# A streaming encoder's MLP: loads at the change to the down product issued by need, and the next norm and the output rows placed inside the last down products' passes

## The chip, the cores and the metric

The kernel runs on one core of a Trainium2 chip. Its time is the device time of one execution in microseconds (us), taken as the median over several runs. Engines are named as the profile names them: PE is TensorE (PEld its weight loads), DVE is VectorE, ACT is ScalarE, POOL is GpSimd, SP is SyncE, whose queue issues nearly all DMA transfers. An instruction on an engine runs when those ahead of it on that engine have run, and when the work it waits for is done.

## The reference

One inference step of a two-layer streaming encoder on 1072 rows of 1024 features: 16 meta tokens, 32 sample rows and 1024 prompt rows. Layer 0 mixes with sliding-window attention beside gated linear attention, layer 1 with forgetting attention. Both layers end in the same MLP, which is what the change is about:

```python
def rmsnorm(x, g):
    xf = x.astype(jnp.float32)
    y = xf * lax.rsqrt(jnp.mean(xf * xf, axis=-1, keepdims=True) + EPS)
    return (y * g.astype(jnp.float32)).astype(x.dtype)

def mlp(h, w_up, w_down):          # w_up 1024 x 4096, w_down 4096 x 1024
    u = jax.nn.relu(h @ w_up)
    return (u * u) @ w_down
...
        xp = xp + mlp(rmsnorm(xp, norm_mlp[l]), w_up[l], w_down[l])
        xs = xs + mlp(rmsnorm(xs, norm_mlp[l]), w_up[l], w_down[l])
    y_prompt = xp[:, N_META:]
```

After layer 0 the rows go through the norm ahead of layer 1's projection; after layer 1 they are the outputs `y_sample` and `y_prompt`, in float32.

## The kernel before

**Layout.** `xT` holds all rows transposed: 128 partitions, 8 feature blocks, 1072 columns, one column for each row. The columns are worked on in four quarters (268 wide in layer 0; 264 in layer 1, which leaves out the meta tokens).

**Precision.** Each float32 product is made of three products of rounded parts: `hi_lo` casts an operand on ACT (line 64: the high part) and subtracts on DVE (line 66: the rest); `mm3` (lines 75 to 77) issues high·high, high·low and low·high. So every operand of TensorE costs one ACT cast and one DVE subtraction first.

**The MLP as seven products.** Each of the two matrix products is done as 2 x 2 blocks with seven block products (a Strassen form with sums S1 to S4 of weight blocks and T1 to T4 of activation blocks). The *up* product runs over 16 blocks of the hidden features; while it runs, `xT` is its scratch memory, so the residual has been spilled to `xsave` in DRAM, and its results go to `ud` in DRAM (the store of line 994). Its operands B11 and B21 lie in the pool `ho1`, the other five in `ho2`.

The *down* product (`down`, from line 1002) follows. For each of seven products n there are two column halves c, so 14 **passes**, written (n, c). A pass runs over 16 blocks kb of 128 hidden features, and for each over 4 output blocks ob with three matmuls: 192 matmuls, 128x268 in layer 0 and 128x264 in layer 1. Results gather in PSUM, in the tile called mu_y for c = 0 and bank for c = 1; at the end of a pass they are added into `xT` (line 1095). Products 0 to 3 give partial sums that go to several outputs; the lower feature half is complete after product 5 and the upper half in parts after products 4, 5 and 6.

**Operands of a pass.** A weight block is loaded as `md_raw` (256 KB, three buffers), combined with blocks that are kept in `md_k` (k1 = A11 and k2 = A21, 4 MB each), and split into `md_w`, one tile for each kb, for the next product while this product's second half runs. The activations come back from `ud` as `md_ur` (two kb at a time, called a group g here; three buffers) and are split into `md_u` (four buffers).

**Order.** TensorE's order inside the MLP is that of the code. Every other engine's order, SP's queue included, is set by a scheduler when the kernel is built.

**At the change to the down product** the code loads k1 (four loads of 1 MB), then for every kb the block A11 a second time as `md_raw` to make `md_w`, and during pass (0, 0) k2 and eight whole-width reloads `xT <- xsave`, two with each megabyte of k2.

**At the end.** In layer 0 the function `done` calls `norm` for quarters 0 and 1 after pass (5, 1), for quarter 2 after (6, 0) and for quarter 3 after (6, 1). `norm` squares the 8 feature blocks on ACT (line 129), adds them on DVE and POOL (line 131), takes the mean over features with one matmul against a constant matrix (line 138), and derives the factor from it; `scaled` then writes the split operand `h` of the projection. In layer 1 `store_rows` takes rows of `xT` through TensorE's transpose (line 1576), copies each half of the features out of PSUM, alternately with ACT (1578) and DVE (1580), and stores it (1581). This is done for the first 544 rows after pass (5, 1), and for 264 rows each after (6, 0) and (6, 1).

Of the kernel before, what the change touches and what calls it, by code (L numbers as in the profile page):

```python
# [8 lines left out]
F32 = mybir.dt.float32  # L9
# [9 lines left out]
P = 128  # L19
D = 1024  # L20
KB = 8
NMETA, NSAMP, NPROMPT = 16, 32, 1024
T = NMETA + NSAMP + NPROMPT
# [6 lines left out]
QMAX = 268  # L30
# [21 lines left out]
class Core:  # L52
# [64 lines left out]

    def squares(self, cols):
        nc, sb = self.nc, self.nm
        c0, c1 = cols  # L120
        w = c1 - c0
        x = self.xT[:, :, c0:c1]

        acc = [sb.tile([P, QMAX], F32, name=f"nm_acc{e}")[:, :w] for e in range(2)]
        for k in range(KB):
            e = k in (1, 3, 5)
            first = k < 2
            sq = acc[e] if first else sb.tile([P, QMAX], F32, name="nm_t", bufs=4)[:, :w]
            nc.scalar.activation(sq, x[:, k], AF.Square)
            if not first:  # L130
                (nc.gpsimd if e else nc.vector).tensor_tensor(acc[e], acc[e], sq, op=ALU.add)
        nc.vector.tensor_tensor(acc[0], acc[0], acc[1], op=ALU.add)
        return lambda: self.normed(w, acc[0])

    def normed(self, w, acc):
        nc, sb = self.nc, self.nm
        ps = self.bank()
        nc.tensor.matmul(ps[:, :w], self.mean, acc, start=True, stop=True)

        y, a = (sb.tile([P, QMAX], F32, name=f"nm_{x}")[:, :w] for x in "ya")  # L140
# [694 lines left out]
    def mlp_begin(self, l):  # L835
        self.l = l
        self.qs = QUARTERS[l]
        self.qw = self.qs[0][1] - self.qs[0][0]
        self.hw = 2 * self.qw
        self.ups = ExitStack()  # L840
        self.ho = {}
        self.operands("ho1", ("B11", "B21"))
        self.xsave = self.dram.tile([P, KB, T], F32, name=f"xsave{l}")

    def operands(self, name, which):
        pool = self.ups.enter_context(self.tc.tile_pool(name=name, bufs=1, side="right", reuse_waits="tile"))
        for x in which:
            self.ho[x] = pool.tile([P, 2, 4, self.hw], F32R, name=f"ho_{x}")
# [152 lines left out]

    def down(self, k1, k2, sb, ps, done):
        nc, i = self.nc, self.i
# [41 lines left out]
        def acts(n, c, g):  # L1045
# [22 lines left out]
        for n, c in passes:  # L1068
# [4 lines left out]
            for kb in range(NP):  # L1073
                if kb % 2 == 0:
                    ready(at)
                    u = us.pop(todo[at])
                    at += 1
                if n == 0 and c == 0 and kb % 4 == 0:
                    load(k2[:, kb:kb + 4], "A21", kb, 4)

                    o = kb // 4
                    for k in (2 * o, 2 * o + 1):
                        nc.sync.dma_start(self.xT[:, k, self.qs[0][0]:], self.xsave[:, k, self.qs[0][0]:])
                for ob in range(4):
# [13 lines left out]

    def mlp(self, after, done):

# [5 lines left out]
        with ExitStack() as st, tc.manual_schedule(engines={mybir.EngineType.PE}):  # L1106
            ps = st.enter_context(tc.tile_pool(name="mlp", bufs=4, space=PSUM, reuse_waits="tile"))
            self.nm = pool(st, "nml")
            self.operands("ho2", ("T4", "B22", "T3", "T2", "T1"))
            with tc.tile_pool(name="mu", bufs=1, reuse_waits="tile") as sb:  # L1110
# [8 lines left out]
            kp = pool(ks, "mk", "right")  # L1119
            k1, k2 = (kp.tile([P, self.NP, 512], F32, name=f"md_k{x}") for x in (1, 2))  # L1120
            sb = pool(st, "md")
            def end(n, c):
                if n == 5 and c == 1:
                    ks.close()
                    after()
                done(n, c)
            self.down(k1, k2, sb, ps, end)

# [439 lines left out]

    def store_rows(self, r0, m):
        nc, o = self.nc, self.o  # L1570
        dst = o["y_sample"][0] if r0 == 16 else o["y_prompt"][0, r0 - 48:r0 - 48 + m]
        for h in range(2):
            y = self.so.tile([P, 512], F32, name="so_y")
            pt = self.bank4()
            for k in range(4):
                nc.tensor.transpose(pt[:m, k], self.xT[:, 4 * h + k, r0:r0 + m], self.ident)
            if h == 0:
                nc.scalar.copy(y[:m], pt[:m].rearrange("p k f -> p (k f)"))
            else:
                nc.vector.tensor_copy(y[:m], pt[:m].rearrange("p k f -> p (k f)"))  # L1580
            nc.sync.dma_start(dst[:, 512 * h:512 * h + 512], y[:m])


def body(tc, i, o):
    C = Core(tc, i, o)
    nc = tc.nc
    with ExitStack() as st:
# [38 lines left out]
        with mixes:  # L1626
# [9 lines left out]
            with tc.tile_pool(name="op2", bufs=6, reuse_waits="tile") as op2:  # L1636
# [14 lines left out]
                for q in range(4):  # L1651
# [3 lines left out]
                    if q < 3:  # L1655
                        C.mlp_norm(q, [steps[q + 1].pop(0) for _ in range(3)])
        hpool = ExitStack()
        nxt = []

        def after():  # L1660
            h = C.projected(hpool.enter_context(right("h2p")), T, 0)
            nxt.extend([h + (0,)] * 3)
# [11 lines left out]
        C.mlp(after, done)  # L1674
        with tc.tile_pool(name="fh0", bufs=1, reuse_waits="tile") as fh0:
# [14 lines left out]
            nm.close()  # L1690
        out = ExitStack()

        def store_space():
            C.so = out.enter_context(tc.tile_pool(name="so", bufs=3, side="right", reuse_waits="tile"))
# [10 lines left out]
        C.mlp(store_space, done)  # L1705
        out.close()

# [66 lines left out]
```

## Time and profile before

| | us |
|---|---|
| median of three runs | 2937.91 (2934.47 to 2941.5) |
| the profiled execution | 2941.2 |
| its span in the trace | 2939.4 |
| PE busy | 2651.7 (90%) |
| DVE busy | 1901.4 (65%) |
| ACT busy | 1262.6 (43%) |
| layer 0: last up matmul to first matmul of the next projection | 974.3 to 1376.0 |
| layer 1: last up matmul to the end of the span | 2539.4 to 2939.4 |

Matmuls overlap in a pipeline, so "busy" does not mean at peak. In a row, the number after the line is an engine's operation, then output<-input by the program's names; brackets give the idle time before it and what ended it. In a row of the waits stand the waiting instruction, the one waited for, the sum, the count and the longest.

### The profile page before, as it was taken

Reading aid. Unit: us, or ns where it says so; the run is one execution under the profiler, and the core shown is the slowest. Engines: PE = TensorE matmul, PEld = TensorE weight load, DVE = VectorE, ACT = ScalarE, POOL = GpSimd, SP = SyncE. Lnnn points to the kernel's source line nnn. Section 1 sums busy time; section 2 is a strip of 40 time slices with the busy share of each in tenths; the row PEclk is TensorE's granted clock in tenths of the full one; section 3 lists DMA queues with packets and bytes.
Section 4 is the critical chain, followed back from the end, with each engine's and each line's share of the span. In section 5 each row is a group of like instructions: output and inputs, shape, how many; then the busy total and the mean of one; then the engine's idle time right before and its main releaser. Section 6 shows DMA issues by size and latency. Waiting matters only on the chain.

```text
span 2939.4 us, 49015 instructions
## 1 busy us (share of the span) xinstructions
PE 2651.7 (90%) x18369; PEld 2457.5 (84%) x18383; DVE 1901.4 (65%) x3867; ACT 1262.6 (43%) x2807; POOL 525.4 (18%) x539
## 2 busy tenths in 40 slices
PE   5899987869999699978999978999978999699998
PEld 5888866769999699968789856778768999699988
DVE  5934467687676386665743556777887676477563
ACT  4345554343333244444433346666653333245342
POOL 3423344100000000002110244555510000000000
PEclk9999988989999799989999979999988999899998
DMA  5343331124443866533465364344223545676543
GB/s 186 104 135 100 89 117 33 57 89 139 147 145 126 327 189 184 148 111 93 118 198 172 114 165 129 86 103 104 66 88 95 158 127 160 258 225 189 171 132 97
DMA packets 369539, 402.15 MB, mean 137 GB/s; under 512 B 41805, under 2 KB 292390, under 8 KB 367254
## 3 DMA queue, kind: packets, MB, share of 16 engines
q1 hardware_dynamic: 366806, 392.01, 45.0%
q0 software_dynamic: 2496, 7.01, 0.7%
q8 instruction: 145, 2.38, 0.3%
q14 instruction: 92, 0.75, 0.1%
HBM read 272.33 MB, written 125.48 MB: 135 GB/s over the span
## 4 chain that ended last, share of the span: by engine, by line
PE 74%; DVE 10%; DMA 7%; ACT 2%; issue 2%; SPq 1%; POOL 0%; DVEq 0%; ACTq 0%
PE bank L75 12%; PE bank L76 12%; PE bank L77 12%; PE mu_y L75 7%; PE mu_y L77 7%; PE mu_y L76 7%; PE bank L1442 2%; DMA md_raw<-in_w_down 2%; DMA md_ur<-ud 2%; PE bank L1452 1%; PE bank L1453 1%; PE fx_s L1424 1%; PE bank L250 1%; PE fx_s L1425 1%; DMA md_k<-in_w_down 1%
## 5 line engine op out<-in xcount | busy, mean ns | idle before, releaser
L75 PE MATMUL mu_y<-md_u,md_w 128*128 128x268 f32 (+1 forms) x896 | 263.0, 294 | 54.3 <-ACT md_u L64 27.8
L75 PE MATMUL bank<-pj_wh,h 128*128 128x384 f32 (+3 forms) x832 | 298.2, 361 | 11.5 <-ACT pj_wh L64 9.1
L77 PE MATMUL bank<-pj_wh,h 128*128 128x384 f32 (+3 forms) x832 | 296.6, 358 | 6.2 <-DVE h L66 4.3
L76 PE MATMUL bank<-pj_wl,h 128*128 128x384 f32 (+3 forms) x832 | 297.6, 359 | 2.5 <-DVE pj_wl L66 2.5
L76 PE MATMUL mu_y<-md_u,md_w 128*128 128x268 f32 (+1 forms) x896 | 260.9, 291 | 0.3 <-DVE md_u L66 0.3
L77 PE MATMUL mu_y<-md_u,md_w 128*128 128x268 f32 (+1 forms) x896 | 261.1, 291 | 0.0
L75 PE MATMUL bank<-md_u,md_w 128*128 128x268 f32 (+1 forms) x896 | 258.2, 288 | 2.9 <-DVE so_y L1580 1.6
L76 PE MATMUL bank<-md_u,md_w 128*128 128x268 f32 (+1 forms) x896 | 256.9, 287 | 1.1 <-DVE md_u L66 1.1
L77 PE MATMUL bank<-md_u,md_w 128*128 128x268 f32 (+1 forms) x896 | 256.7, 286 | 0.0
L66 DVE TENSOR_TENSOR md_u<-md_ur,md_u 128x536 fp32r<-128x536 f32 (+1 forms) x224 | 159.4, 715 | 135.4 <-ACT md_u L64 131.7
L64 ACT CAST md_u<-md_ur 128x536 fp32r<-128x536 f32 (+1 forms) x224 | 141.8, 635 | 222.4 <-PE mu_y L77 121.5
L75 PEld LDWEIGHTS mu_y<-md_u,md_w 128*128 128x128 f32 x896 | 174.6, 195 | 55.7 <-ACT md_u L64 28.3
L76 PE MATMUL mu_y<-ho_T,mu_w 128*128 128x268 f32 (+1 forms) x768 | 219.8, 286 | 0.5 <-DVE ho_T L66 0.5
L75 PE MATMUL mu_y<-ho_T,mu_w 128*128 128x268 f32 (+1 forms) x768 | 220.3, 287 | 0.0
L77 PE MATMUL mu_y<-ho_T,mu_w 128*128 128x268 f32 (+1 forms) x768 | 219.9, 286 | 0.0
L66 DVE TENSOR_TENSOR mu_w<-mu_raw,mu_w 128x512 fp32r<-128x512 f32 x160 | 110.2, 689 | 117.4 <-ACT mu_w L64 117.4
L1255 POOL TENSOR_TENSOR fx_p<-fx_p,sm_den 128x144 f32<-128x144 f32 (+7 forms) x128 | 150.7, 1178 | 184.5 <-DVE sm_den L1254 168.7
L64 ACT CAST mu_w<-mu_raw 128x512 fp32r<-128x512 f32 x160 | 99.1, 622 | 187.5 <-PE bank L77 125.0
L75 PEld LDWEIGHTS bank<-pj_wh,h 128*128 128x128 f32 x832 | 159.3, 192 | 24.0 <-ACT pj_wh L64 9.6
L76 PEld LDWEIGHTS mu_y<-md_u,md_w 128*128 128x128 f32 x896 | 174.6, 195 | 1.0 <-DVE md_u L66 0.9
L77 PEld LDWEIGHTS mu_y<-md_u,md_w 128*128 128x128 f32 x896 | 174.3, 194 | 1.1 <-DVE md_w L66 1.1
L77 PEld LDWEIGHTS bank<-pj_wh,h 128*128 128x128 f32 x832 | 159.1, 191 | 18.1 <-DVE h L66 4.9
(530 smaller groups left out, 8064.5 us busy)
## 6 DMA issues: line engine op xcount, KB each, us to landing
md_raw<-in_w_down SPq DMA_DIRECT2D x192, 256.0 KB
mu_raw<-in_w_up SPq DMA_DIRECT2D x64, 512.0 KB
ud<-xT SPq DMA_DIRECT2D x16, 1876.0 KB
md_ur<-ud SPq DMA_DIRECT2D x112, 268.0 KB
ud<-xT SPq DMA_DIRECT2D x16, 1848.0 KB
md_ur<-ud SPq DMA_DIRECT2D x112, 264.0 KB
md_k<-in_w_down SPq DMA_DIRECT2D x16, 1024.0 KB
fh_ka<-zk SPq DMA_DIRECT2D x32, 260.0 KB
```

The costliest lines, as they stand in the source:

```text
L64: nc.scalar.copy(hi, src)
L66: nc.vector.tensor_tensor(lo, src, hi.bitcast(F32), op=ALU.subtract)
L75: mm(out, ah, bh, start=start, stop=False)
L76: mm(out, ah, bl, start=False, stop=False)
L77: mm(out, al, bh, start=False, stop=stop)
L250: nc.tensor.matmul(*args, start=k == x == 0, stop=k == KB - 1 and x == 1)
L1255: nc.gpsimd.tensor_tensor(p[:, :n], p[:, :n], den[:, 0:1].to_broadcast([P, n]), op=ALU.mult)
L1424: nc.tensor.matmul(s[:, a:b], qa[:, qc], ka[:, t0 + a:t0 + b], start=True, stop=False)
L1425: nc.tensor.matmul(s[:, a:b], qb[:, qc], kb[:, t0 + a:t0 + b], start=False, stop=ma >= mb)
L1442: nc.tensor.transpose(pt[:m, P * j:P * j + P], pr[j][:, k0:k0 + m], self.ident)
L1452: nc.tensor.matmul(po[:, c], vt[:m, t], th[:m, c], start=t == 0, stop=False)
L1453: nc.tensor.matmul(po[:, c], vt[:m, t], tl[:m, c], start=False, stop=t == 4 * quad + 4)
```

## The change

1. `md_k` becomes eight tiles of four kb each, so that each load is awaited by itself. The weights of product 0 are made from k1; the second load of A11 is gone (32 loads of 256 KB less over the two layers).
2. The loads of k2 and the reloads of `xT` are each put `behind` an activation block: a one-element POOL copy from that `md_u` tile into the load's target, which the load must follow. k2 comes in four megabytes at kb 2, 6, 10 and 14 of pass (0, 0); `xT` comes by quarter and feature half, two loads in each pass of products 0 to 3 at kb 4.
3. The pool `ho2` moves to the other side of on-chip memory, with its blocks in another order, so that the tiles of `md_k` lie over `ho1`, whose last readers are early products of the last up block.
4. The norm after layer 0 is cut up. Quarters 0 and 1 are squared after passes (4, 0) and (4, 1), quarter 2 by feature halves after (5, 1) and (6, 0), quarter 3 partly within (6, 1). Their mean matmuls stand inside passes (5, 0), (5, 1) and (6, 1), behind kb 5. Only quarter 3's other half, its mean and its scaling come after the last pass.
5. The output rows of layer 1 are stored in half rows (24 pieces), one behind each odd kb of the passes from (4, 1) on. All copies are on ACT, and `so_y` has two buffers instead of three.

```diff
     def down(...):
             x = self.DOWN[n][0]
-            a, b = k1[:, kb], k2[:, kb]
-            src = None
-            if x == "S2":
+            a, b = (k[kb // 4][:, kb % 4] for k in (k1, k2))
+            if x == "A11":
+                src = a
+            elif x == "S2":
...
+        def behind(dst, u):
+            nc.gpsimd.tensor_copy(dst, u[0:1, 0, 0, 0:1].bitcast(F32))
+
         for x in range(4):
-            load(k1[:, 4 * x:4 * x + 4], "A11", 4 * x, 4)
+            load(k1[x], "A11", 4 * x, 4)
...
-                if n == 0 and c == 0 and kb % 4 == 0:
-                    load(k2[:, kb:kb + 4], "A21", kb, 4)
-
-                    o = kb // 4
-                    for k in (2 * o, 2 * o + 1):
-                        nc.sync.dma_start(self.xT[:, k, self.qs[0][0]:], self.xsave[:, k, self.qs[0][0]:])
+                if n == 0 and c == 0 and kb % 4 == 2:
+                    x = k2[kb // 4]
+                    behind(x[0:1, 0, 0:1], u)
+                    load(x, "A21", kb - 2, 4)
+
+                if n < 4 and kb == 4:
+                    c0, c1 = self.qs[2 * (int(to[0][1]) - 1) + c]
+                    f = 4 * (int(to[0][0]) - 1)
+                    for k in range(f, f + 4, 2):
+                        for j in (k, k + 1):
+                            behind(self.xT[0:1, j, c0:c0 + 1], u)
+                        nc.sync.dma_start(self.xT[:, k:k + 2, c0:c1], self.xsave[:, k:k + 2, c0:c1])
...
+                bank = self.bank
+                if c:
+                    self.bank = lambda: ps.tile([P, 512], F32, name="mu_y")
+                mid(n, c, kb)
+                self.bank = bank
...
-            self.operands("ho2", ("T4", "B22", "T3", "T2", "T1"))
+            self.operands("ho2", ("T1", "T2", "T3", "T4", "B22"), "left")
...
 # layer 0
+        def mid(n, c, kb):
+            if n == 5 and kb == 5:
+                row(c)
+            elif (n, c, kb) == (6, 1, 5):
+                row(2)
+                normal(2)
+                some(3, range(4, 8))
...
         def done(n, c):
-            if n < 5 or (n, c) == (5, 0):
-                return
-            for q in ((0, 1) if n == 5 else (2 + c,)):
-                c0, c1 = QUARTERS[0][q]
-                y = C.norm((c0, c1))
-                hi, lo, h = nxt[0][:3]
-                C.scaled(2, C.xT[:, :, c0:c1], y, C.nm, (hi[:, :, c0:c1], lo[:, :, c0:c1], h), q == 0)
+            if n == 4:
+                some(c, range(KB))
+            elif (n, c) == (5, 1):
+                h = C.projected(hpool.enter_context(right("h2p")), T, 0)
+                nxt.extend([h + (0,)] * 3)
+                normal(0)
+                normal(1)
+                some(2, range(4, 8))
+            elif (n, c) == (6, 0):
+                some(2, range(4))
...
 # layer 1
+        def mid(n, c, kb):
+            if kb % 2 and todo:
+                C.store_rows(*todo.pop(0))
 
         def done(n, c):
-            if (n, c) == (5, 1):
-                C.store_rows(16, 32)
-                for r0, m in ((48, 128), (176, 128), (304, 128), (432, 112)):
-                    C.store_rows(r0, m)
+            if n == 4:
+                todo.extend((*r, h) for r in rows[c] for h in range(2))
+            elif n == 5:
+                todo.extend((*r, 1) for r in rows[2 + c])
             elif n == 6:
-                for r in range(3):
-                    C.store_rows(544 + 264 * c + 88 * r, 88)
+                todo.extend((*r, 0) for r in rows[2 + c])
+            while c and n == 6 and todo:
+                C.store_rows(*todo.pop(0))
```

In `some(q, ks)` the squares and sums of the given feature blocks are made, in `row(q)` the mean matmul and the factor, in `normal(q)` the scaling.

**SP's queue at layer 0's change to the down product**, from the last but one store of the up results on (`ud<-xT`). Before:

```order
L994 DMA ud_6543<-xT 128x3752 x2
L1083 DMA xT<-xsave_5904 128x1072 x4
L1010 DMA md_k_10197<-in_w_down 128x4x512 x4
L1010 DMA md_raw<-in_w_down 128x512 x3
L1049 DMA md_ur<-ud_6540 128x2x268 x2
L994 DMA ud_6543<-xT 128x3752
L1049 DMA md_ur<-ud_6541 128x2x268
L1010 DMA md_k_10198<-in_w_down 128x4x512 x4
L1010 DMA md_raw<-in_w_down 128x512 x3
```

and after:

```order
L1001 DMA ud_6543<-xT 128x3752 x2
L1018 DMA md_k_10197<-in_w_down 128x4x512
L1018 DMA md_k_10198<-in_w_down 128x4x512
L1018 DMA md_k_10199<-in_w_down 128x4x512
L1018 DMA md_k_10200<-in_w_down 128x4x512
L1058 DMA md_ur<-ud_6540 128x2x268 x2
L1058 DMA md_ur<-ud_6541 128x2x268
L1018 DMA md_raw<-in_w_down 128x512 x2
L1001 DMA ud_6543<-xT 128x3752
L1018 DMA md_raw<-in_w_down 128x512
L1018 DMA md_k_10201<-in_w_down 128x4x512
```

The four reloads of `xT` and the second load of A11 are gone from ahead of the first activations, and A21 (the last row) is one megabyte at a time. The `md_raw` of the new queue are blocks of the next product's weights.

**DVE at the same place**, from the up product's last sums (line 993, now 1000) on. Before:

```order
L993 TENSOR_TENSOR xT<-xT 128x536 x4
L66 TENSOR_TENSOR md_w_10208<-md_raw,md_w_10208 128x512
L66 TENSOR_TENSOR md_w_10213<-md_raw,md_w_10213 128x512
L66 TENSOR_TENSOR md_w_10218<-md_raw,md_w_10218 128x512
L66 TENSOR_TENSOR md_u<-md_ur,md_u 128x536 x3
```

and after (the rows left out are ten more of the kind of their neighbours):

```order
L1000 TENSOR_TENSOR xT<-xT 128x536 x4
L66 TENSOR_TENSOR md_w_10212<-md_k_10197,md_w_10212 128x512
L66 TENSOR_TENSOR md_w_10215<-md_k_10197,md_w_10215 128x512
L66 TENSOR_TENSOR md_w_10218<-md_k_10197,md_w_10218 128x512
...
L66 TENSOR_TENSOR md_w_10251<-md_k_10200,md_w_10251 128x512
L66 TENSOR_TENSOR md_w_10254<-md_k_10200,md_w_10254 128x512
L66 TENSOR_TENSOR md_w_10257<-md_k_10200,md_w_10257 128x512
L66 TENSOR_TENSOR md_u<-md_ur,md_u 128x536 x3
```

Three weight blocks were split ahead of the first activations; now all 16 are, on DVE as on ACT.

**TensorE at the end of the passes.** Layer 0 before, at the end of pass (5, 1), and after, inside pass (5, 0):

```order
L77 MATMUL bank<-md_u,md_w_13125 128x268
L138 MATMUL bank<-nm_acc_13722,mean 128x268
L138 MATMUL bank<-nm_acc_13797,mean 128x268
L75 MATMUL mu_y<-md_u,md_w_13400 128x268
```

```order
L77 MATMUL mu_y<-md_u,md_w_12991 128x268
L145 MATMUL bank<-nm_acc_12862,mean 128x268
L75 MATMUL mu_y<-md_u,md_w_13011 128x268
```

And layer 1 after, inside pass (4, 1), where one piece of four transposes stands between two kb:

```order
L77 MATMUL bank<-md_u,md_w_29656 128x264
L1603 MATMUL mu_y<-ident,xT 32x128 x4
L75 MATMUL bank<-md_u,md_w_29678 128x264
```

The matmuls of mean and transpose have moved from a pass's end to within passes.

More of the change, by code (lines that the diff above doesn't have):

```diff
@@ L118, in squares, with some_squares @@
     def squares(self, cols):
+        return self.some_squares(cols, range(KB))[1]
+    def some_squares(self, cols, ks, so_far=None):
         nc, sb = self.nc, self.nm
@@ L122, in squares @@
         x = self.xT[:, :, c0:c1]
[L124 to L127, printed above, removed]
+        acc, at = so_far[0] if so_far else ([sb.tile([P, QMAX], F32, name=f"nm_acc{e}")[:, :w] for e in range(2)], 0)
+        for k in ks:
+            e = at in (1, 3, 5)
+            first = at < 2
+            at += 1
             sq = acc[e] if first else sb.tile([P, QMAX], F32, name="nm_t", bufs=4)[:, :w]
@@ L841, in mlp_begin, with operands @@
         self.ho = {}
-        self.operands("ho1", ("B11", "B21"))
+        self.operands("ho1", ("B11", "B21"), "right")
         self.xsave = self.dram.tile([P, KB, T], F32, name=f"xsave{l}")
-    def operands(self, name, which):
-        pool = self.ups.enter_context(self.tc.tile_pool(name=name, bufs=1, side="right", reuse_waits="tile"))
+    def operands(self, name, which, side):
+        pool = self.ups.enter_context(self.tc.tile_pool(name=name, bufs=1, side=side, reuse_waits="tile"))
         for x in which:
@@ L1096, in down, with mlp @@
             done(n, c)
-    def mlp(self, after, done):
+    def mlp(self, nms, mid, done):
         tc, nc = self.tc, self.nc
@@ L1119, in mlp @@
             kp = pool(ks, "mk", "right")
-            k1, k2 = (kp.tile([P, self.NP, 512], F32, name=f"md_k{x}") for x in (1, 2))
+            k1, k2 = ([kp.tile([P, 4, 512], F32, name=f"md_k{x}{y}") for y in range(4)] for x in (1, 2))
             sb = pool(st, "md")
+            if self.l:
+                self.so = pool(st, "so", bufs=2)
             def end(n, c):
@@ L1124, in end @@
                     ks.close()
-                    after()
                 done(n, c)
-            self.down(k1, k2, sb, ps, end)
+            self.down(k1, k2, sb, ps, mid, end)
     def project_c(self, hT, beside):
@@ L1566, in fox, with store_rows @@
                     self.mlp_norm(q, [steps[q + 1].pop(0) for _ in range(3)])
-    def store_rows(self, r0, m):
+    def store_rows(self, r0, m, h):
         nc, o = self.nc, self.o
         dst = o["y_sample"][0] if r0 == 16 else o["y_prompt"][0, r0 - 48:r0 - 48 + m]
[L1572 to L1581, printed above, removed]
+        y = self.so.tile([P, 512], F32, name="so_y")
+        pt = self.bank4()
+        for k in range(4):
+            nc.tensor.transpose(pt[:m, k], self.xT[:, 4 * h + k, r0:r0 + m], self.ident)
+        nc.scalar.copy(y[:m], pt[:m].rearrange("p k f -> p (k f)"))
+        nc.sync.dma_start(dst[:, 512 * h:512 * h + 512], y[:m])
 def body(tc, i, o):
@@ L1690, in body @@
             nm.close()
-        out = ExitStack()
-        def store_space():
-            C.so = out.enter_context(tc.tile_pool(name="so", bufs=3, side="right", reuse_waits="tile"))
+        nms = ExitStack()
+        rows = [[(16, 32), (48, 116), (164, 116)]] + [[(280 + 264 * q + 88 * r, 88) for r in range(3)] for q in range(3)]
+        todo = []
+        def mid(n, c, kb):
+            if kb % 2 and todo:
+                C.store_rows(*todo.pop(0))
         def done(n, c):
-            if (n, c) == (5, 1):
-                C.store_rows(16, 32)
-                for r0, m in ((48, 128), (176, 128), (304, 128), (432, 112)):
-                    C.store_rows(r0, m)
+            if n == 4:
+                todo.extend((*r, h) for r in rows[c] for h in range(2))
+            elif n == 5:
+                todo.extend((*r, 1) for r in rows[2 + c])
             elif n == 6:
-                for r in range(3):
-                    C.store_rows(544 + 264 * c + 88 * r, 88)
-        C.mlp(store_space, done)
-        out.close()
+                todo.extend((*r, 0) for r in rows[2 + c])
+            while c and n == 6 and todo:
+                C.store_rows(*todo.pop(0))
+        C.mlp(nms, mid, done)
+        nms.close()
 def constants():
```

31 lines of the change are left out of this document (21 added, 10 removed).

## The prediction

> **What bounds the kernel now.** I read the page first, then both down products in stretches of time, then in each stretch the waits and the order in time. From the page, the span and the chain that ended last:
>
> ```profile
> span 2939.4 us, 49015 instructions
> PE 74%; DVE 10%; DMA 7%; ACT 2%; issue 2%; SPq 1%; POOL 0%; DVEq 0%; ACTq 0%
> ```
>
> TensorE (PE) holds 74% of that chain; the other 26% are held by something else while TensorE waits. Where, the stretches tell (columns: from and to, length, then busy us and instructions of PE, its weight loads, DVE, ACT and POOL, granted clock, DMA share, GB/s):
>
> ```profile
> 974.40:1032.20 57.80, 32.20 (x195) 30.71 (x194) 21.73 (x33) 16.24 (x27) 0.00 (x0) 0.70 0.97 344
> ...
> 1056.00:1293.30 237.30, 237.30 (x1922) 237.30 (x1920) 158.67 (x265) 108.28 (x186) 1.84 (x2) 1.00 0.57 164
> 1293.30:1316.60 23.30, 1.63 (x7) 0.89 (x6) 21.50 (x49) 11.04 (x26) 5.07 (x7) 0.62 0.27 77
> 1316.60:1376.00 59.40, 51.40 (x388) 50.38 (x386) 31.18 (x58) 22.65 (x52) 13.80 (x15) 0.95 0.23 59
> 2539.50:2598.50 59.00, 29.96 (x195) 28.50 (x194) 21.70 (x33) 16.53 (x27) 0.00 (x0) 0.77 0.97 343
> 2598.50:2623.60 25.10, 23.98 (x195) 23.48 (x194) 25.10 (x44) 11.43 (x19) 0.00 (x0) 1.00 0.66 202
> 2623.60:2856.60 233.00, 233.00 (x1922) 233.00 (x1920) 152.73 (x256) 103.62 (x175) 0.00 (x0) 1.00 0.56 164
> 2856.60:2873.50 16.90, 8.49 (x43) 6.41 (x41) 13.94 (x27) 6.30 (x11) 0.00 (x0) 0.70 0.51 156
> 2873.50:2939.40 65.90, 56.00 (x435) 54.55 (x432) 16.89 (x28) 12.17 (x20) 0.00 (x0) 0.93 0.31 92
> ```
>
> A pass has 192 matmuls. Ten undisturbed passes take 237.30 us in layer 0 (23.73 each) and 233.00 in layer 1 (23.30 each). What the other stretches take beyond their passes is lost, in four places:
>
> - start of layer 0, one pass in 57.80: **34.1 us**
> - end of layer 0, two passes in 23.30 + 59.40 = 82.70: **35.2 us**
> - start of layer 1, two passes in 59.00 + 25.10 = 84.10: **37.5 us**
> - end of layer 1 with the kernel's tail, two passes in 16.90 + 65.90 = 82.80: **36.2 us**
>
> At the starts the DMA engines are busy 97% and TensorE about half; at the ends the DMA engines have room.
>
> **The change: start of the down products.** TensorE's waits in both first stretches (us in total, times, longest), and SP's queue in layer 0:
>
> ```profile
> PE mu_y L75 <- ACT md_u L64: 13.8, 1, 13.8
> PE mu_y L75 <- ACT md_w L64: 11.6, 2, 9.5
> ...
> PE mu_y L75 <- ACT md_w L64: 14.9, 2, 10.8
> PE mu_y L75 <- ACT md_u L64: 14.0, 1, 14.0
> ...
> 965.07 1.75 SPq L1083 DMA_DIRECT2D xT<-xsave  x4
> 966.92 5.42 SPq L1010 DMA_DIRECT2D md_k<-in_w_down  x4
> 972.38 5.28 SPq L1010 DMA_DIRECT2D md_raw<-in_w_down  x3
> ...
> 985.03 7.99 SPq L1010 DMA_DIRECT2D md_k<-in_w_down  x4
> ```
>
> The first weights (md_raw) queue behind four xT reloads and 4 MB of md_k, which holds the same block A11; then 4 MB of A21 and four more xT reloads hold up the next md_raw, which is the second wait, 9.5 and 10.8 us. After the change the first weights are cut from md_k itself, at the queue's head, and A21 and xT come by need. So what is late next? The order shown above tells: all 16 weight casts, and all 16 subtractions on DVE, stand ahead of the first md_u. DVE and ACT at the end of the up product, and the weights' price:
>
> ```profile
> 971.68 0.40 ACT L976 ACTIVATE xT<-mu_y 128x268 f32<-128x268 f32 x1 [1.10 <-PE mu_y L77]
> 985.65 1.96 ACT L64 CAST md_w<-md_raw 128x512 fp32r<-128x512 f32 x3 [13.58 <-DMA md_raw<-in_w_down]
> ...
> 977.87 0.72 DVE L993 TENSOR_TENSOR xT<-xT 128x536 f32<-128x536 f32 x1
> 986.30 2.03 DVE L66 TENSOR_TENSOR md_w<-md_raw,md_w 128x512 fp32r<-128x512 f32 x3 [7.71 <-ACT md_w L64]
> 988.44 1.37 DVE L66 TENSOR_TENSOR md_u<-md_ur,md_u 128x536 fp32r<-128x536 f32 x2
> ...
> 2540.95 2.69 DVE L993 TENSOR_TENSOR xT<-xT 128x528 f32<-128x528 f32 x4
> ```
>
> ACT: 972.1 + 16 × 0.65 (1.96 for three) puts the first md_u cast near 983. DVE finishes the up product's sums at 978.6, then 16 × 0.677 (2.03 for three) = 10.8 and 0.7 for the first md_u: 990.1. The second matmul needs that, so the first wait does not shrink at all: 15.7 us from 974.4. In layer 1 2543.6 + 10.8 + 0.7 = 2555.1, or 15.6. A faster spacing of 0.63 would give 15.0.
>
> The restart costs beside the wait, since the granted clock is 0.70 and 0.77 there:
>
> ```profile
> 989.61 0.43 PE L77 MATMUL mu_y<-md_u,md_w 128*128 128x268 f32 x1
> ...
> 994.97 0.30 PE L77 MATMUL mu_y<-md_u,md_w 128*128 128x268 f32 x1
> ```
>
> 24 issues lie between these rows: 5.36 us, where 24 × 0.1236 (23.73 / 192) = 2.97 would do. With the slow pair before them I take 2.8 us for a restart. [...]
>
> Behind the restart I expect no second wait. Some 7 MB (4 MB of A21, eight md_ur of 0.27, xT pieces) over a pass of 23.7 us are 290 GB/s, and 344 went through in the first stretch. Activations are cast up to four groups of 2.97 us (23.73 / 8) ahead of TensorE. An in-order load behind a POOL copy needs a cast, a copy and its issue, some 2 us, and a 1 MB block ahead of it 3 more (at 344 GB/s). So I price the new waits on SP at 0, covered by that lead; if the lead is gone, a late group costs up to its 2.97 us, 24 us for the eight of a pass.
>
> Layer 0: 34.1 − 15.7 − 2.8 = **15.6 us** gained. Layer 1: 37.5 − 15.6 − 2.8 = **19.1**, the second pass's 1.8 included.
>
> **The change: end of layer 0.** The longest wait of the first stretch, and PE before and after the last pass:
>
> ```profile
> PE bank L138 <- DVE nm_acc L132: 17.6, 1, 17.6
> ...
> 1346.70 0.81 PE L138 MATMUL bank<-nm_acc,mean 128*128 128x268 f32 x1 [4.82 <-DVE nm_acc L132]
> ...
> 1376.01 0.52 PE L75 MATMUL bank<-pj_wh,h 128*128 128x272 f32 x2 [3.18 <-ACT pj_wh L64]
> ```
>
> The mean matmuls stand at a pass's end and wait for squares that begin only then. Now three of the four stand 72 matmuls (8.9 us) into a later pass, with their squares a pass or half a pass before. The moved work is the same: 21.50 us of DVE and 11.04 of ACT in the stretch of 23.30, now over five passes (118.7 us) in which DVE is busy two thirds (158.67 of 237.30), ACT less than half. So it is covered; uncovered, a mean that is late costs what the quoted one did, about 5 us. Inside the passes remain the three matmuls, 0.4 us each, 1.2 in all. Behind the last pass remain the last quarter's adds and half its squares ahead of the weights' cast: I keep the whole 3.5 us, and 0.6 for a restart. 35.2 − 1.2 − 4.1 = **29.9 us** gained.
>
> **The change: end of layer 1.** Transposes, copies and stores, first wait and tail:
>
> ```profile
> 2863.07 1.04 PE L1576 MATMUL bank<-ident,xT 128*32 128x128 f32 x4 [6.26 <-DVE xT L1095]
> ...
> 2929.30 3.18 PE L1576 MATMUL bank<-ident,xT 128*88 128x128 f32 x24
> 2930.33 0.58 ACT L1578 COPY so_y<-bank 88x512 f32<-88x512 f32 x1 [11.81 <-PE bank L1576]
> 2930.93 4.96 SPq L1581 DMA_DIRECT2D out_y_prompt<-so_y  x6
> 2933.44 0.69 DVE L1580 COPY so_y<-bank 88x512 f32<-88x512 f32 x1 [1.99 <-DMA out_y_prompt<-so_y]
> 2934.88 0.69 DVE L1580 COPY so_y<-bank 88x512 f32<-88x512 f32 x1 [0.76 <-DMA out_y_prompt<-so_y]
> ```
>
> 21 half rows now lie within passes: 84 transposes at 0.13 (3.18 / 24) = 11 us, 9 if the pitch is 0.11; I take 10, and 1.2 for small waits on PSUM. Three half rows stay behind the end where six were: two copies, the third waits for the first store (at 2933.44 as before), and ends at 2934.0 rather than 2935.6, so the tail of 9.9 us (2929.5 to 2939.4) shrinks by 1.6 to 8.3. 36.2 − 10 − 1.2 − 8.3 = **16.7 us** gained. The price if cover fails is the first rival below.
>
> **The change: start of the up product, layer 0.** With the operands on the other side of memory the first mu_raw loads wait for the last scaling on DVE:
>
> ```profile
> 604.05 6.50 SPq L896 DMA_DIRECT2D mu_raw<-in_w_up  x4
> ...
> 610.73 3.74 DVE L866 SCALAR_TENSOR_TENSOR xT<-xT,gain,nm_y 128x268 f32<-128x268 f32 x8
> ...
> 622.42 0.59 PE L77 MATMUL mu_y<-ho_B,mu_w 128*128 128x268 f32 x1 [3.06 <-DVE mu_w L66]
> ```
>
> Issued at 614.5 instead of 604.1, 1 MB for the first block lands some 3 us later (at 344 GB/s), near 618, and DVE reaches the first mu_w only for the matmul at 622.42. Cost between 0 and 3; I take **0.5**.
>
> **Sum.** 15.6 + 19.1 + 29.9 + 16.7 − 0.5 = 80.8 us. From the profiled execution's 2941.2 (its span of 2939.4 and 1.8 around it) that is 2860.4; from the median of the runs, 2937.9, 2857.1. I say **2859**.
>
> **The rivals.**
>
> *The half rows stall the passes; slower than before.* Copies now stand on ACT alone, ahead of the md_u casts in its queue, and SP's store ahead of the next md_ur. With two buffers a copy waits for the store two pieces back. One piece comes per two kb, 2.97 us and its 0.5, so two pieces give 6.9 us; a store took 2933.4 − 2930.9 = 2.5 and a copy 0.6. It decides once a store takes over 6.3 us; beyond that 21 pieces pay each excess, and 81 us of gain are gone at 6.3 + 3.9 = 10.2 us a store. Against it: DMA shares of 0.31 and 0.51 in these stretches. At 10.5 us a store the time would be 2946. Chance 0.05 with the stores between, 0.01 of it for an end within 0.2%.
>
> *A second wait stays at the starts.* SP is in order, and now stands at POOL copies which wait for casts. If the wait for weights is only exchanged for one for md_u, the starts gain nothing: 34.7 less, 2894; a half of it, 2876. For it: POOL's adds beside DVE's took between 749 and 3063 ns:
>
> ```profile
> L131 POOL TENSOR_TENSOR nm_acc<-nm_acc,nm_t x24: 749/890/3063, 567.3 to 2188.5; 128x268 f32<-128x268 f32 x16, 128x264 f32<-128x264 f32 x8
> ```
>
> So a copy on POOL may take some 2 us more than it should; 36 a layer, each ahead of a load. [...] The lead of three to four groups takes up 2 us, so I give 0.12.
>
> *The norm stalls inside passes.* Each of three means late by 5 us, with a restart, is 3 × (5 + 2) = 21: 2880; one of them, 2867. Chance 0.14.
>
> *The changed loads don't come early.* Should md_k wait for the up product's last matmul (974.4), its 4 MB take 12 us at 344 GB/s, to 986.6; the last cast, four subtractions and the md_u then end near 991, 1 us later than I say, in either layer: 2861, within the forecast.
>
> *More than I say.* If DVE interleaves the weights earlier and the restart is short, the starts gain 4 us more each, and the tail 3: 2848 and less. Chance 0.07.
>
> **How the numbers follow.** The forecast, 2848 to 2872, has 0.62; the norm's stalls 0.14; the second wait 0.12; more gain 0.07; the half rows 0.05. The predicted time is the forecast's. The range of 2846 to 2884 leaves out the worse half of the second wait, the half rows, and the far end of more gain, together some 0.15. This kernel's measurement can tell about 0.2%, 6 us, from no change. All cases but the last lie faster by over 40 us: faster 0.95, the same 0.01, slower 0.04.
>
> **What would show it.** In the changed kernel's trace: TensorE idle about 15 to 16 us before each down product's second matmul, released by DVE md_u, with no wait for md_w after it; twelve passes of 23.7 and 23.3 us with nothing between; mean matmuls without a wait in front; transposes of 0.5 us between kb; a tail of 8.3 us. I am wrong if a first pass of either layer is over 29 us from its second matmul, if a pass from the fifth to the seventh product is over 26, or if the first wait is under 12 or over 19 us.

## The result, and the profile after

| | before | changed |
|---|---|---|
| median of four runs, us | 2939.7 (2934.47 to 2942.91) | 2861.93 (2855.66 to 2869.08) |
| ratio | | 0.9738 (95% interval 0.9707 to 0.9768) |
| profiled execution, span | 2941.2, 2939.4 | 2855.66, 2853.9 |

The change makes the kernel 2.6% faster, 78 us. 2859 was predicted, with a range of 2846 to 2884. That the two times lie 3 us apart is partly luck: in the table of losses below, one term was missed by 4.9 us, and three smaller misses lie on the other side.

The chain that ended last, of the changed kernel (the profile's page):

```profile
span 2853.9 us, 49119 instructions
PE 63%; issue 16%; DVE 9%; DMA 3%; ACT 2%; SPq 1%; POOL 1%; DVEq 0%; ACTq 0%; POOLq 0%
```

DMA fell from 7% to 3%; PE and "issue" (time in which the engine waited for nothing that the profile shows) together hold 79% where they held 76%.

The stretches that answer to those of before (from and to, length, busy us and instructions of PE, weight loads, DVE, ACT, POOL, granted clock, DMA share, GB/s):

```profile
972.70:1013.70 41.00, 26.88 (x196) 26.15 (x195) 29.38 (x48) 14.83 (x26) 3.57 (x8) 0.79 1.02 370
1013.70:1326.70 313.00, 310.29 (x2504) 309.64 (x2502) 223.45 (x399) 151.28 (x282) 35.25 (x52) 1.00 0.58 167
2485.30:2526.60 41.30, 26.11 (x194) 25.40 (x194) 29.87 (x49) 14.76 (x26) 3.93 (x8) 0.83 1.03 369
2526.60:2713.00 186.40, 186.40 (x1538) 186.40 (x1537) 127.75 (x215) 85.32 (x145) 13.08 (x28) 1.00 0.68 203
2713.00:2853.90 140.90, 129.86 (x1058) 128.22 (x1057) 64.51 (x112) 53.52 (x93) 0.00 (x0) 0.98 0.43 123
```

Undisturbed passes still take 23.73 and 23.30 us (eight in 186.40). So the first pass of layer 0 has 41.00 − 23.73 = 17.3 us over, and that of layer 1 41.30 − 23.30 = 18.0. The other thirteen passes of layer 0, up to the next projection, take 313.0, which is 13 × 23.73 and 4.5. The last five of layer 1 with the tail take 140.9, which is 5 × 23.30 and 24.4.

| loss, us | before | predicted | measured |
|---|---|---|---|
| start, layer 0 | 34.1 | 18.5 | 17.3 |
| start, layer 1 | 37.5 | 18.4 | 18.0 |
| end, layer 0 | 35.2 | 5.3 | 4.5 |
| end, layer 1, with the tail | 36.2 | 19.5 | 24.4 |
| sum | 143.0 | 61.7 | 64.2 |

78.8 us of the spans' difference of 85.5 lie in these four places. The remaining 6.7 lie outside: 1.7 ahead of the first start, 3.0 between the next projection's first matmul and layer 1's first up matmul, where the code is as before, and 1.8 in layer 1's up product; 0.2 is rounding. The stretch of the 3.0 took between 810 and 817 us in the ten profiles of this study, so that part is the spread of executions. The profiled one was also the fastest of the four.

### The profile page after: what moved, and what is told of

It is laid out like the page before. It is cut to its first block, busy times and chain, and to the rows that moved or that the text cites. A ratio compares the mean times of both kernels' runs of the same rounds, so it can differ in the third digit from the quotient of the medians.

```text
span 2853.9 us, 49119 instructions
## 1 busy us (share of the span) xinstructions
PE 2631.2 (92%) x18391; PEld 2440.6 (86%) x18391; DVE 1888.3 (66%) x3856; ACT 1264.4 (44%) x2820; POOL 560.7 (20%) x611
## 4 chain that ended last, share of the span: by engine, by line
PE 63%; issue 16%; DVE 9%; DMA 3%; ACT 2%; SPq 1%; POOL 1%; DVEq 0%; ACTq 0%; POOLq 0%
PE bank L75 11%; PE bank L76 11%; PE bank L77 11%; PE mu_y L77 5%; PE mu_y L76 5%; PE mu_y L75 5%; PE bank L1470 2%; PE bank L1480 1%; PE bank L1481 1%; PE fx_s L1452 1%; PE fx_s L1453 1%; DMA md_raw<-in_w_down 1%; PE bank L257 1%; DVE gl_Q L600 1%; PE b L701 1%
## 5 line engine op out<-in xcount | busy, mean ns | idle before, releaser
L75 PE MATMUL mu_y<-md_u,md_w 128*128 128x268 f32 (+1 forms) x896 | 259.4, 289 | 26.9 <-ACT md_u L64 26.9
L76 PE MATMUL mu_y<-md_u,md_w 128*128 128x268 f32 (+1 forms) x896 | 257.8, 288 | 2.4 <-DVE md_u L66 2.4
L77 PE MATMUL mu_y<-md_u,md_w 128*128 128x268 f32 (+1 forms) x896 | 257.3, 287 | 0.0
L75 PEld LDWEIGHTS mu_y<-md_u,md_w 128*128 128x128 f32 x896 | 171.1, 191 | 27.4 <-ACT md_u L64 27.3
L76 PEld LDWEIGHTS mu_y<-md_u,md_w 128*128 128x128 f32 x896 | 170.9, 191 | 3.5 <-DVE md_u L66 3.4
L76 PEld LDWEIGHTS bank<-pj_wl,h 128*128 128x128 f32 x832 | 159.0, 191 | 16.3 <-DVE pj_wl L66 5.2
```

The source lines that it names most:

```text
L75: mm(out, ah, bh, start=start, stop=False)
L76: mm(out, ah, bl, start=False, stop=False)
L77: mm(out, al, bh, start=False, stop=stop)
```

## The experiments

Each is an edit of the changed kernel unless it says otherwise; the kernel before ran beside all of them. "Start" and "end" are the losses of the table above, layer 0 first, in each experiment's own profile. A start runs from the start of the last up matmul over the first pass, and over the second where that loses time too.

**The start alone.** The kernel before with the new loads and memory sides only (parts 1 to 3 of the change); the norm and the output rows are those of before. The edit is shown against the kernel before.

```diff
-            a, b = k1[:, kb], k2[:, kb]
-            src = None
-            if x == "S2":
+            a, b = (k[kb // 4][:, kb % 4] for k in (k1, k2))
+            if x == "A11":
+                src = a
+            elif x == "S2":
...
-            load(k1[:, 4 * x:4 * x + 4], "A11", 4 * x, 4)
+            load(k1[x], "A11", 4 * x, 4)
...
+                    behind(x[0:1, 0, 0:1], u)
...
-            self.operands("ho2", ("T4", "B22", "T3", "T2", "T1"))
+            self.operands("ho2", ("T1", "T2", "T3", "T4", "B22"), "left")
```

> The loads at the change to the down product and the memory sides as in the changed kernel; the norm and the output rows as before. My reading (the two halves of the change are independent): of 79 us found in the two traces' down products, 16.9 + 19.5 = 36.4 belong to the starts and 42.6 to the ends, so about 2903 us, with both starts at 17 and 18 us over an undisturbed pass and the ends at 35 and 36 as before. Rival (the gains overlap, e.g. the passes after a faster start run into something): less than 30 us, over 2910.

Measured: 2903.28 us, ratio 0.9892 (0.9875 to 0.9909). Starts 19.4 and 20.0, ends 35.8 and 33.9. The time is the expected one, but the kernel before took 2935.52 us beside it, so the gain is 32 us and not the 36.4 that were expected: the starts are 2 us longer in each layer than in the changed kernel, in part by a second wait that is told of at the exchange of md_k's halves, below.

**The end alone.** The changed kernel with the loads and memory sides of before.

```diff
-            a, b = (k[kb // 4][:, kb % 4] for k in (k1, k2))
-            if x == "A11":
-                src = a
-            elif x == "S2":
+            a, b = k1[:, kb], k2[:, kb]
+            if x == "S2":
...
-                if n == 0 and c == 0 and kb % 4 == 2:
+                if n == 0 and c == 0 and kb % 4 == 0:
+                    load(k2[:, kb:kb + 4], "A21", kb, 4)
...
-            self.operands("ho2", ("T1", "T2", "T3", "T4", "B22"), "left")
+            self.operands("ho2", ("T4", "B22", "T3", "T2", "T1"), "right")
```

> The norm and the output rows as in the changed kernel; loads and memory sides as before. My reading: starts as before (34 and 37 us over an undisturbed pass), ends as in the changed kernel (4.5 us in layer 0, 24 in layer 1 with the tail), so 42 us gained, about 2897. Rival (the ends only fit because of the later xT loads or the other memory side): ends over 10 us longer than in the changed kernel, 2907 or more.

Measured: 2891.64 us, ratio 0.9851 (0.9834 to 0.9868). Starts 34.5 and 38.3, ends 3.4 and 21.2. The two ratios multiply to 0.9745; both together gave 0.9738. Within these intervals the halves of the change are independent, and the ends bring the larger part.

**Not by need.** The POOL copies left out, so that A21 and xT load as early as their memory allows; A11 still loaded once.

```diff
-                    behind(x[0:1, 0, 0:1], u)
...
-                        for j in (k, k + 1):
-                            behind(self.xT[0:1, j, c0:c0 + 1], u)
```

> The changed kernel without the POOL copies: A21 and xT are loaded as early as their memory is free, A11 still once. The order built puts eight xT pieces (2.1 MB) ahead of md_k, and A21 ahead of the fourth activation block. If loading by need is what shortens the starts: the first weights come some 5 us later and a second wait appears before the fourth activation group, 6 to 12 us more in each layer than in the changed kernel (17 and 18). Rival (the 4 MB of A11 that are not loaded twice do it): 17 to 20 us, as in the changed kernel.

Measured (one run): 2875.58 us; starts 29.3 and 28.4. TensorE's waits in the first stretch, and SP's queue:

```profile
PE mu_y L75 <- ACT md_u L64: 22.6, 2, 16.0
...
968.36 4.02 SPq L1018 DMA_DIRECT2D md_k<-in_w_down  x4
972.43 5.72 SPq L1058 DMA_DIRECT2D md_ur<-ud  x3
978.19 3.39 SPq L1018 DMA_DIRECT2D md_k<-in_w_down  x2
981.69 1.62 SPq L1001 DMA_DIRECT2D ud<-xT  x1
983.41 3.34 SPq L1018 DMA_DIRECT2D md_k<-in_w_down  x2
986.80 7.82 SPq L1018 DMA_DIRECT2D md_raw<-in_w_down  x3
994.71 2.38 SPq L1058 DMA_DIRECT2D md_ur<-ud  x3
```

There are two waits for activations, the longer of 16.0 us; the second matmul comes 17.3 us after the last up matmul, 2.6 later than in the changed kernel, where the expectation had some 5. The other wait, 6.6 us, is for the fourth activation block, which is issued at 994.71, behind 4 MB of A21.

**A11 twice.** Loads by need, but the first weights from a second load of A11, as before.

```diff
-            if x == "A11":
-                src = a
-            elif x == "S2":
+            if x == "S2":
```

> The changed kernel, but with A11 loaded a second time as md_raw for the first weights, as before the change; A21 and xT by need. If the bytes ahead of the first operands set the starts: the first md_raw follow 4 MB of md_k, so the first wait is 14 to 15 us as in both kernels, and the rest of md_raw (3.3 MB more in the first pass) adds waits of 3 to 8 us: 20 to 26 us over an undisturbed pass where the changed kernel has 17 and 18. Rival (loading by need does it all): 17 to 19.

Measured (one run): 2881.71 us; starts 30.5 and 31.8. The expectation named the right sign and too small a size, and so missed its range of 20 to 26. The waits:

```profile
PE mu_y L75 <- ACT md_u L64: 14.0, 1, 14.0
PE mu_y L75 <- ACT md_w L64: 7.5, 2, 4.4
```

So neither half of the new loading does it alone: in layer 0 loading once without need leaves 29.3 of the 34.1 us, need without loading once 30.5, both together 17.3. Each removes bytes that stand ahead of what the first pass needs next, and while either stays the pass still waits for a load.

**md_k's halves exchanged in memory.**

```diff
-            k1, k2 = ([kp.tile(...) for y in range(4)] for x in (1, 2))
+            k2, k1 = ([kp.tile(...) for y in range(4)] for x in (2, 1))
```

> The changed kernel with md_k's two halves exchanged in memory, so that k1 lies where ho1 was. In the changed kernel's trace the first md_k load waited until 970.03, for the matmuls of T4, and the third until 972.99, for those of B22. My reading: the four loads now issue at about 958 to 962, the weight casts on ACT are done earlier, but DVE still begins its 16 subtractions only when the up product's sums are done, so the second matmul of the down product comes no more than 0.5 us earlier: start of layer 0 stays at 17 us over an undisturbed pass, layer 1 at 18. Rival (the loads are the limit): it comes up to 8 us earlier in each layer, when the casts follow the up product's end at once.

The reason for this run is a mistake in what stands ahead of the prediction: md_k's tiles were said to lie over `ho1`, whose readers are done early. That holds for k2 only. k1, which is needed first, lies over T4 and B22 of `ho2`, the last operands that the up product reads. SP's wait and issues in the changed kernel:

```profile
SPq L1018 <- PE mu_y L77: 10.0, 1, 10.0
...
970.03 3.88 SPq L1018 DMA_DIRECT2D md_k<-in_w_down  x4
973.95 3.27 SPq L1058 DMA_DIRECT2D md_ur<-ud  x3
```

After the exchange (its SP queue, the end of DVE's up sums and weights, and TensorE's first two matmuls of the down product):

```profile
958.15 5.93 SPq L1018 DMA_DIRECT2D md_k<-in_w_down  x4
970.18 3.84 SPq L1058 DMA_DIRECT2D md_ur<-ud  x3
...
977.00 9.71 DVE L66 TENSOR_TENSOR md_w<-md_k,md_w 128x512 fp32r<-128x512 f32 x16
986.64 1.96 DVE L66 TENSOR_TENSOR md_u<-md_ur,md_u 128x536 fp32r<-128x536 f32 x3
...
979.49 0.59 PE L75 MATMUL mu_y<-md_u,md_w 128*128 128x268 f32 x1 [6.38 <-ACT md_u L64]
987.40 0.59 PE L76 MATMUL mu_y<-md_u,md_w 128*128 128x268 f32 x1 [7.32 <-DVE md_u L66]
```

The loads go out 12 us earlier, and the first matmul follows 7 us earlier. The second comes, behind DVE, as late as before: 14.6 us after the last up matmul (972.82), 14.7 in the changed kernel. Time 2856.55 (one run); starts 16.2 and 16.0, 1 to 2 us less than in the changed kernel. Part of the difference is a second wait, at the fourth activation block; the rest is lost less behind the waits. The second wait is 0.3 and 1.2 us in the changed kernel, 1.9 and 1.8 in the run of the start alone, 1.6 and 1.6 in the run with the later half rows below, all three with the same loads; after the exchange it is absent. So the early loads take away this small wait and leave the first.

**Activations ahead of most weights.** The first three md_ur loads are put behind the first md_k load.

```diff
-        for x in range(4):
-            load(k1[x], "A11", 4 * x, 4)
+        load(k1[0], "A11", 0, 4)
...
+        ready(0)
+        for x in range(1, 4):
+            load(k1[x], "A11", 4 * x, 4)
         for kb in range(NP):
             w[0, kb] = weights(0, kb)
```

> The changed kernel with the first three md_ur loads put behind the first md_k load, ahead of the other three; the built order then has 4 weight blocks ahead of the first md_u on ACT and DVE instead of 16. My reading (the queue of weights ahead of the first activation sets the wait): DVE is free at 976.9, 4 x 0.61 + 0.65 later the second matmul starts, near 980.0 instead of 987.35, and no later wait appears: 7 us less in each layer, 14 together, about 2848. Rival (loads set the pace, 1 MB each 2.7 us for four blocks): the later weights come too late, a new wait appears inside the first pass and less than 3 us is gained in a layer.

Measured: 2861.7 us, ratio 0.9748 (0.9728 to 0.9767), the changed kernel's time; starts 19.6 and 20.9. My reading fell and the rival held. The second matmul does come at 980.8, as worked out, but a new wait follows at 991.3. TensorE's waits in layer 0's first pass, SP's queue and ACT:

```profile
PE mu_y L75 <- ACT md_u L64: 10.6, 2, 5.6
PE mu_y L76 <- DVE md_u L66: 3.2, 2, 1.7
...
972.96 2.28 SPq L1018 DMA_DIRECT2D md_k<-in_w_down  x3
975.29 2.92 SPq L1018 DMA_DIRECT2D md_raw<-in_w_down  x2
978.32 0.57 SPq L1001 DMA_DIRECT2D ud<-xT  x1
978.93 0.89 SPq L1018 DMA_DIRECT2D md_raw<-in_w_down  x1
979.92 0.50 SPq L1018 DMA_DIRECT2D md_k<-in_w_down  x1
981.06 2.00 SPq L1058 DMA_DIRECT2D md_ur<-ud  x1
...
996.47 0.64 ACT L64 CAST md_u<-md_ur 128x536 fp32r<-128x536 f32 x1 [7.86 <-DMA md_ur<-ud]
```

The fourth activation block is issued at 981.06 and cast at 996.47, when it has landed: 15 us for 268 KB. Ahead of it stand 4096 KB of A11, 804 of activations, 768 of md_raw, 1876 of the up product's last store and 1024 of A21, together 8.8 MB from 970.8 on, and at the 370 GB/s of the changed kernel's first stretch these would take 24 us, to 995 (an estimate). It was not weights that came too late, as the rival had it, but bytes in the queue all the same. So there are two limits which end within a few us of each other: DVE's chain of 16 weight blocks, and the bytes ahead of the fourth activation block. Lifting either alone moves the wait, not the end.

**No half row right after pass (5, 1).** In layer 1's pass (6, 0) the three pieces stand behind kb 5, 7 and 9 instead of 1, 3 and 5.

```diff
-            if kb % 2 and todo:
+            if kb % 2 and todo and (n, c, kb) not in ((6, 0, 1), (6, 0, 3)):
                 C.store_rows(*todo.pop(0))
```

> The changed kernel with one edit: no half row behind kb 1 and 3 of layer 1's pass (6, 0), so that pass's three pieces stand behind kb 5, 7 and 9. My reading of the wait of 4 to 5.5 us at the first piece of that pass: its rows need the sums of pass (5, 1), and these stand on DVE behind a subtraction that waits for a load of md_raw; four kb (5.8 us) later they are there. So pass (6, 0) falls from 31.4 to about 25 us with no wait before a transpose, 5 to 6 us less in all. Rival (the pass is short of DVE or of weights, and the wait only moves): pass (6, 0) stays over 29 us, with the time waited for md_u or md_w.

In the changed kernel the first piece of that pass waits (TensorE, then DVE, then SP):

```profile
2796.71 0.65 PE L1603 MATMUL bank<-ident,xT 128*88 128x128 f32 x2 [4.02 <-DVE xT L1120]
...
2794.68 0.69 DVE L1043 TENSOR_TENSOR md_raw<-md_raw,md_k 128x512 f32<-128x512 f32 x1 [0.62 <-DMA md_raw<-in_w_down]
2795.29 0.69 DVE L66 TENSOR_TENSOR md_w<-md_raw,md_w 128x512 fp32r<-128x512 f32 x1
2795.89 2.80 DVE L1120 TENSOR_TENSOR xT<-xT,bank 128x264 f32<-128x264 f32 x8
...
2790.11 3.69 SPq L1018 DMA_DIRECT2D md_raw<-in_w_down  x2
```

Pass (5, 1) ended at 2789.6, yet its sums (L1120) start at 2795.89, because they stand on DVE behind subtractions that wait for md_raw loads. Moved back, the piece finds them done. Pass (6, 0) of the edited kernel as one stretch, and the only wait of TensorE from there to the end:

```profile
2793.90:2820.30 26.40, 24.93 (x206) 24.73 (x205) 15.79 (x30) 9.87 (x17) 0.00 (x0) 1.00 0.54 155
...
PE mu_y L76 <- DVE md_u L66: 1.5, 1, 1.5
```

26.4 us instead of 31.4, and no transpose waits. 2853.77 us, ratio 0.9714 (0.9700 to 0.9727). The interval overlaps the changed kernel's, so the gain of 5 us is read from the pass and not from the times.

**All limits at once.** md_k's halves exchanged, the late half rows, and the weights of kb 4 to 15 made only after the first activation block, by a one-element POOL copy into each of their tiles.

```diff
-        def weights(n, kb):
+        def weights(n, kb, u=None):
...
             hl = sb.tile([P, 2, 512], F32R, name=f"md_w{kb}", bufs=1)
+            if u is not None:
+                behind(hl[0:1, 0, 0:1], u)
...
-        for kb in range(NP):
+        for kb in range(4):
             w[0, kb] = weights(0, kb)
+        ready(0)
+        for kb in range(4, NP):
+            w[0, kb] = weights(0, kb, us[todo[0]])
```

> The changed kernel with three edits: md_k's halves exchanged in memory (the four loads early), the weights of kb 4 to 15 made only after the first activation block (a one-element POOL copy into each of their tiles), and the late half rows. The exchange alone gave 1 to 2 us a layer, activations ahead alone 0. My reading (two limits that end within 1 us of each other: DVE's chain of 16 weight blocks, and the 8.5 MB queued ahead of the fourth activation block): with both gone the second matmul of each down product starts about 7 us after the up product's last instead of 14.5, no second wait: starts of 10 to 11 us instead of 17 and 18, and with the late half rows about 20 us less than the changed kernel, 2842. Rival (there is a third limit as close): starts stay over 14 us.

Measured: 2840.01 us, ratio 0.9671 (0.9652 to 0.969), the fastest kernel of this study. The first passes of both layers, and TensorE's waits in layer 0:

```profile
975.40:1008.60 33.20, 26.37 (x195) 25.56 (x194) 26.88 (x45) 12.78 (x22) 12.27 (x20) 0.90 0.98 353
2486.70:2519.00 32.30, 25.88 (x194) 25.37 (x194) 26.82 (x45) 12.44 (x22) 11.96 (x20) 0.89 1.00 359
...
PE mu_y L75 <- ACT md_u L64: 5.2, 1, 5.2
PE mu_y L76 <- DVE md_u L66: 1.7, 2, 1.3
PE bank L76 <- DVE md_u L66: 1.0, 1, 1.0
```

The first pass has 9.5 and 9.0 us over instead of 17.3 and 18.0; with 1.6 and 1.8 us lost in the second pass the starts are 11.1 and 10.9. By itself the exchange was worth 1 to 2 us in a layer, and the activations ahead of most weights, brought about by another edit in that run, cost 2 to 3; both limits lifted together give 6 to 7 us in each layer. The rival of a third limit as close, with starts over 14 us, did not come true.

## Why the prediction was right, and where it was not

*The start: right in size, half right in cause.* That the first wait would not shrink, because all 16 weight blocks stand ahead of the first md_u on DVE, holds. The second matmul starts 14.7 and 14.9 us after the last up matmul, where 15.7 and 15.6 were worked out:

```profile
976.85 9.82 DVE L66 TENSOR_TENSOR md_w<-md_k,md_w 128x512 fp32r<-128x512 f32 x16
986.59 1.96 DVE L66 TENSOR_TENSOR md_u<-md_ur,md_u 128x536 fp32r<-128x536 f32 x3
...
983.53 2.18 ACT L64 CAST md_w<-md_k 128x512 fp32r<-128x512 f32 x4 [0.57 <-DMA md_k<-in_w_down]
985.61 1.71 ACT L64 CAST md_u<-md_ur 128x536 fp32r<-128x536 f32 x3
```

The 16 subtractions start 0.61 us apart. I had taken 0.677 from three that ran behind ACT's casts, and so counted ACT's pace as DVE's. The step "ACT puts the first md_u cast near 983" failed: it came at 985.61, since the loads started at 970.03. This was the rival of loads that don't come early, which I had priced at 1 us. It came true in the main and cost nothing in the end, because DVE finished its weights 1 us after ACT. The step "I price the new waits on SP at 0, covered by that lead" failed, at a small price: at the fourth activation block there was no lead. TensorE's waits for DVE in the first stretches of layers 0 and 1, one of each two at the second matmul (0.5 us) and one at that block, and ACT in layer 0:

```profile
PE mu_y L76 <- DVE md_u L66: 0.8, 2, 0.5
PE mu_y L76 <- DVE md_u L66: 1.6, 2, 1.2
...
995.85 0.65 ACT L64 CAST md_u<-md_ur 128x536 fp32r<-128x536 f32 x1 [8.52 <-DMA md_ur<-ud]
```

ACT casts the block when it has landed, at 995.85; DVE has subtracted it at 998.83, and TensorE had come to it at 998.29. The second wait is 0.3 us in layer 0 and 1.2 in layer 1. The bytes ahead of that block, which I had only averaged over the pass, decided as soon as the first wait was shortened.

*The restart.* The first pass of layer 0 has 17.3 us over, 14.7 of them up to the second matmul, which leaves 2.6; in layer 1 18.0 − 14.9 = 3.1. I had taken 2.8 from the row, but the second wait is in these figures. Without it 2.3 and 1.9 are left for the restart, and after the exchange, where no second wait came, 1.6 and 1.5. So the size was about right in sum and too large as the price of a restart. In the changed kernel matmuls 0.22 us apart follow the second one from 987.74 to 991.76 in layer 0 and from 2500.54 to 2503.84 in layer 1, 4.0 and 3.3 us, with a granted clock of 0.50 there (987.35 to 992.00, 2500.10 to 2502.50). The row quoted of before, with slow matmuls from 989.61 to 994.97 (5.4 us, granted clock 0.50), was a long case.

*The end of layer 0: right in sum, by two misses that partly cancel.* 4.5 us remain where 5.3 were predicted. Passes (5, 0) and (5, 1), with one mean matmul each, are 24.18 us, 0.45 over; (6, 1) is 1.5 over, 0.8 of it a wait of its mean for DVE. That makes 2.4 us within passes where I had 1.2. Behind the last pass 2.1 remain where I had kept 4.1. No run shows the 0.6 us in it for a restart: in the changed kernel TensorE is idle for 1.9 us there, and the granted clock of the stretch is 1.00 (1299.4 to 1326.7).

*The end of layer 1: 16.7 predicted, 11.8 measured.* The step that failed is "1.2 for small waits on PSUM": TensorE shows no wait for PSUM there, and one for sums in its place. The 21 pieces cost 0.45 us each (passes of 26.01 with six pieces against 23.31), 9.5 where 10 were worked out, and the tail was as predicted: 8.2 us from the first transpose of the last three pieces to the end, 8.3 predicted. But the first piece after pass (5, 1) waited for DVE's sums, 4.6 us in three waits, and with the restart behind them (granted clock 0.72 from 2798.5 to 2803.0) pass (6, 0) has 6.7 us over beside its pieces. At 31.4 us it is over the 26 that I had named as a sign of being wrong. The row was there: I had quoted the transpose at 2863.07 with "6.26 <-DVE xT L1095" and counted that wait as gone, because pieces move. The first piece of every pass stands two kb, 2.9 us, behind the end of the pass ahead, whose sums it needs. In the other passes these sums were done 0.6 to 1.9 us after that end; here they began 6.3 us after it and were done after 9.1 (2789.6 to 2798.7). The run without that piece gained 5.0 us in the stretch.

*The start of the up product: nothing.* The loads go out at 614.46, as worked out, and the second matmul starts at 622.21 instead of 622.42. The 0.5 us were not needed.

*The rivals.* Stalling half rows: a store took 2.3 us in the tail, far from the 6.3 at which it decides, and the passes with half rows show no wait for `so_y`. A second wait at the starts came true, but at 0.3 and 1.2 us of the 34.7 that it was priced at. Of the norms inside passes one mean waited, 0.8 us. The slower side was nowhere near.

## What to carry to other kernels

When a load is moved to the front of a phase, work out the order of *everything* that stands between it and the first matmul, on each engine and in bytes on the queue: here DVE's 16 weight blocks and 8.8 MB of transfers ended so close together that lifting one moved the wait and not the end. Where a piece of work is placed inside a pass, count its distance from the point at which the other engines' queues reach its inputs, and not from the matmuls that these inputs come from. And a rate that is taken from a row should come from a stretch in which that engine, not its supplier, was the limit.

## What the runs showed of the hardware

The one-element POOL copies are not free. Their durations in the changed kernel (ns: least, median, most), and one place in its order of time, on POOL, DVE and SP:

```profile
L1064 POOL COPY xT<-md_u x64: 173/174/4267, 987.4 to 2665.3; 1x1 f32<-1x1 f32 x64
L1064 POOL COPY md_k<-md_u x8: 414/526/727, 986.8 to 2522.3; 1x1 f32<-1x1 f32 x8
...
1035.88 4.62 POOL L1064 COPY xT<-md_u 1x1 f32<-1x1 f32 x4 [15.78 <-ACT md_u L64]
...
1039.41 0.70 DVE L66 TENSOR_TENSOR md_u<-md_ur,md_u 128x536 fp32r<-128x536 f32 x1
1040.04 0.76 DVE L1120 TENSOR_TENSOR xT<-xT,bank 128x268 f32<-128x268 f32 x2
1040.29 0.87 SPq L1102 DMA_DIRECT2D xT<-xsave  x2
```

Of the 72 copies 40 took 0.17 to 0.18 us. When they began, DVE was idle, ran sums that read PSUM (line 1120), or had at most 0.13 us left of an instruction with both inputs in SBUF. The other 32 took longer, and each ended 0.03 to 0.04 us after the end of such a DVE instruction: 30 took 0.41 to 0.78 us, one 4.27, and one in layer 1 3.90. During the first of the two long ones DVE ran seven instructions with two inputs in SBUF without a gap (1035.77 to 1040.11, the last of them quoted), and the copy ended at 1040.15, beside one that reads PSUM. SP issued the xT loads at 1040.29, right after, with md_ur behind them from 1041.72 on. The first activation block of these was split at 1048.56, and TensorE came to it at 1049.29. So TensorE did not wait, but 0.7 us were left of the lead of three to four groups, 2.97 us each, that the prediction counted on. Here a copy that holds back a load was safe by that lead alone, and the lead was all but used up.

In kernels with `ho2` on the other side of memory layer 1's up product took 348 to 349 us; before, and in the run of the end alone, it took 350.5. The difference lies in its longest wait, near the start, 10.4 to 11.3 us instead of 13.1, while the wait ahead of its first matmul is longer, 4.7 to 5.8 instead of 4.0. The cause was not looked into.
